# A Macaron transformer block on one core: seven products for the attention's values, plain tiles for x, and p2 on m1's bank

## The chip, the cores and the metric

The kernel runs on one core of a Trainium2 chip. The metric is the device time of one execution in microseconds. The kernel before took 1191.23 us, the median of 3 runs (1188.14 to 1192.05).

## What is computed

One block for 512 positions of 1024 features, all in float32: half a SwiGLU feed-forward block, a mixer of a short convolution and gated linear attention with four heads, half another feed-forward block, and a final RMS norm. Cut to what matters:

```python
D_MODEL, SEQ, D_FF = 1024, 512, 2816
GLA_HEADS, GLA_DK, GLA_DV, CHUNK = 4, 128, 256, 64

def swiglu(x, w_gu, w_down):
    g, u = jnp.split(x @ w_gu, 2, axis=-1)
    return (jax.nn.silu(g) * u) @ w_down

def hybrid_mixer(h, ...):
    z = h @ w_in
    cb, cc, cu, q, k, v, g_lr, r, ga, gb = jnp.split(z, SPLIT_POINTS, axis=-1)
    y_conv = (cb * causal_short_conv(cc * cu, conv_w)) @ w_out_conv
    log_a = jax.nn.log_sigmoid(g_lr @ gate_w_up + gate_b) / GATE_TAU
    o = gla_chunked(q, k, v, log_a)          # per head: decayed scores, states, outputs
    o = o * lax.rsqrt(jnp.mean(o * o, axis=-1, keepdims=True) + EPS)
    y_gla = (o.reshape(B, S, GLA_V) * gla_norm_g * jax.nn.silu(r)) @ w_out_gla
    merged = jax.nn.sigmoid(ga) * y_conv + jax.nn.sigmoid(gb) * y_gla
    return merged @ w_o

x = x + 0.5 * swiglu(rmsnorm(x, norm_ffn1_g), ffn1_w_gu, ffn1_w_down)
x = x + hybrid_mixer(rmsnorm(x, norm_mix_g), ...)
x = x + 0.5 * swiglu(rmsnorm(x, norm_ffn2_g), ffn2_w_gu, ffn2_w_down)
return rmsnorm(x, final_norm_g)
```

## The kernel before

**Matmuls.** Activations are kept transposed (features on the 128 partitions, the 512 positions beside them) in one large tile `X` of eight blocks. Each float32 operand is split into a high part, a ScalarE cast (L309 for a weight, into `wh`), and a low part, a VectorE subtraction (L310, into `wl`). A product is then three matmuls: high by high, high by low, low by high.

**Products and sets.** A *single* or a *group* is a plain product over all eight blocks of features. Most of the weights, though, go through *sets* of seven half-size products (the scheme of Strassen and Winograd), named m1, p2, q6, p5, q7, p4, p3. In an ordinary set (`Set.run`, matmuls at L501) one product is 24 matmuls of 128 by 256. Three PSUM banks take them: m1, then q6, q7 and p4 into b, p2 into a, p5 and p3 into c. What stands in b after m1, q6 and q7 is copied to SBUF by ScalarE (L506) before the next product writes there, and VectorE combines it later with another bank: m1 with p2's bank a, q6 and q7 with bank c. `order()` interleaves neighbours: the following set's m1 runs just before this set's p4, and its p2 between p4 and p3. The down projections use *wide* sets: matmuls of 128 by 512, two weight tiles to a product, order m1, p5, q6, p2, q7, p3, p4.

**Weights.** `PLAN` lists the tiles to load, `STEPS` the products that use them, in the order of use. `Weights.issue` runs two steps ahead of TensorE (PE): it casts and subtracts for a product, and asks for later loads. A set needs four loads and one sum tile, out of a pool `f` of ten tiles of 512 KB, so a load waits until an older tile is free. SyncE's queue (SP) issues the loads. They are asked for six steps ahead of the set's m1, and the sums of sub-blocks three steps ahead: s3 = a11 + a21 on VectorE; a21 += a22, and after the casts of m1 and p2, a11 += a21 and a12 += a11, as adding DMAs of GpSimd's queue (POOL, L287). Tiles of singles and groups are asked for by `fetch` a few steps ahead (four in the mixer). Each engine takes its instructions in a fixed order, by and large that in which they were written; DMA issues of SP may stand earlier.

**The mixer**, in its order on PE: the group of queries and keys of heads 0 and 1, with the gates' low-rank product; the values' first half (`v_half(0)`, by `mm_wide`: 96 matmuls of 128 by 512, L378 and others, recorded as L337 to L339 and L378 by form); singles for the queries and keys of heads 2 and 3, with the scores, state and output of head 0 between them; `v_half(1)`; twelve sets in the order of `MSETS` (ga and gb are the gates, conv the convolution, cb its gate, r the output gate) with the work of heads 1 to 3 hooked behind chosen products; w_out_conv in eight singles; two sets of w_out_gla; w_o. A head's work runs through `gates` (L1058 is its matmul on PE), `decays` (a scan and four exponentials, each function of ScalarE behind a table load), `scale`, `scores`, `state`, `output`, `squares`.

The matmuls of the values' halves read x as it is before the division by its root mean square; keys are therefore scaled by the square of that row (`row2`). The sets read `X` after VectorE has normalized it in place (L1032). Old x lies in device memory (`xs`) meanwhile: `reload`, a hook behind p3 of the first w_out_gla set, reads it into a new large tile with eight DMAs of POOL's queue (L1453), and `evac` (L1458) adds w_o's product to it.

Of the kernel before, what the change touches and what calls it, by code (L numbers as in the profile page):

```python
# [15 lines left out]
P = 128  # L16
S = 512
# [39 lines left out]


def wide(mat, kt, col):
    return [(mat, k0, 2, (col,), 512) for k0 in range(0, kt, 2)]  # L60
# [61 lines left out]
MSETS = [("ga", 0), ("gb", 0), ("conv", 0), ("ga", 1), ("conv", 1), ("gb", 1), ("conv", 2),  # L122
# [19 lines left out]
def ffn_plan(up, down, plain, slow):  # L142
# [6 lines left out]
    wide_sets(down)  # L149
# [4 lines left out]
def mixer_plan():  # L154
    units(group("w_in", KD, (QO, KO, QO + P, KO + P)))
    units(wide("w_in", KD, VO))
# [3 lines left out]
    units(wide("w_in", KD, VO + 512))  # L160
# [23 lines left out]
def block_kernel(ctx: ExitStack, tc: tile.TileContext, xT, vecs, gf, gup, wgl, wts, out):  # L184
# [58 lines left out]
    class Weights:  # L243
# [13 lines left out]
        def phase(self, early, first=6):  # L257
# [4 lines left out]
            for i in range(lo, self.end):  # L262
                n, p = STEPS[i]
                if p == "m1":
                    self.loads.setdefault(max(lo, i - first), []).append(n)
# [4 lines left out]
        def fetch(self, at):  # L270

            for n, p in STEPS[at : min(at + self.early, self.end)]:
# [78 lines left out]
    def mm_group(mat, kt, cols, ah, al, extra=None, slow=False):  # L351
        o = [MM() for _ in cols]
        n = len(cols)
        for u in group(mat, kt, cols, slow):
            h, l = W.take(u)
            for i in range(u[2]):
# [6 lines left out]
                if extra is not None:  # L363
                    extra(k)
        return o

    def mm_wide(mat, kt, col, ah, al, extra=None):
        o = [MM() for _ in range(NTB)]
        for u in wide(mat, kt, col):
            h, l = W.take(u)  # L370
            for i in range(u[2]):
                k = u[1] + i
                wh = h[:, i * 512 : (i + 1) * 512]
                wl = l[:, i * 512 : (i + 1) * 512]
                for t in range(NTB):
                    a = ah[k][:, t * P : (t + 1) * P]
                    b = al[k][:, t * P : (t + 1) * P]
                    nc.tensor.matmul(o[t], a, wh, start=k == 0, stop=False)  # L378
                    nc.tensor.matmul(o[t], a, wl, start=False, stop=False)
                    nc.tensor.matmul(o[t], b, wh, start=False, stop=k == kt - 1)  # L380
# [97 lines left out]
    class Set:  # L478
# [8 lines left out]
        def run(self, p):  # L487
# [16 lines left out]
            if p in ("m1", "q6", "q7"):  # L504
# [3 lines left out]
            self.done(self, p)  # L508

# [84 lines left out]

    def run_sets(make, ahead=2, hooks={}):
# [8 lines left out]
        for n, i in number.items():  # L604
            sets[n] = make(i)
        for i, (n, p) in enumerate(seq):
# [7 lines left out]
    def ffn(up, down, norm, nxt, plain, at):  # L614
# [917 lines left out]
```

## Time and profile before

| what | value |
|---|---|
| median of 3 runs | 1191.23 us |
| the profiled execution's own time | 1192.07 us |
| its span, first to last instruction | 1190.4 us |
| mean granted TensorE clock | 0.997 |
| first matmul of the mixer | at 343.2 us |
| first matmul of w_o | at 800.6 us |

All times on the page are within the span; 1.67 us of the profiled execution lie around it. In a row of a group, the numbers behind the bar are its busy time in us, the mean of one in ns, and the idle time of the engine just before its instructions with what ended it. In a row of a timeline, the first number is the start in us, the second how long the instruction was open, and the bracket behind it the idle time before it and its releaser. In the chain of waits, a row gives when a stretch of work began, how long it lasted, and the engine and line.

### The profile page before, as it was taken

The numbers are of one execution on the slowest core, as the hardware profiler recorded it, in microseconds if no ns is written. First come the engines' busy times: TensorE is split into PE (matmuls) and PEld (weight loads), VectorE is DVE, ScalarE is ACT, GpSimd is POOL, SyncE is SP. The second block draws the span as 40 slices with busy tenths as digits, with TensorE's granted clock in tenths as the row PEclk, the third lists the DMA queues.
The fourth block names the chain that finished last, engine by engine and source line by source line (L and its number), as shares of the span: only waits on it lengthen the run. The fifth ranks groups of instructions, "written<-read, shape, count | busy, mean of one in ns | idle before, by whom it ended". The sixth has DMA issues, their size and how long they took to land. (4 is left out here: it accounts for less than half of the span.)

```text
span 1190.4 us, 19195 instructions
## 1 busy us (share of the span) xinstructions
PE 1177.9 (99%) x7818; PEld 1085.6 (91%) x7818; DVE 878.5 (74%) x1044; ACT 625.5 (53%) x777; POOL 116.3 (10%) x155
## 2 busy tenths in 40 slices
PE   9999999999999999999999999999999999999997
PEld 8899999988788889999999998988889999998876
DVE  7976666897578765868688688676598666679955
ACT  6564454675245465646454566543345454566543
POOL 0011111101010001011111100200001101101100
PEclk9999999999999999999999999999999999999999
DMA  9477777678532325766877766741537777757721
GB/s 349 85 207 187 183 181 191 153 196 209 195 110 85 89 71 149 205 179 178 206 218 176 189 181 200 208 128 54 186 72 210 173 193 176 182 156 192 170 81 71
DMA packets 61224, 197.10 MB, mean 166 GB/s; under 512 B 6768, under 2 KB 13040, under 8 KB 61136
## 3 DMA queue, kind: packets, MB, share of 16 engines
q0 software_dynamic: 18560, 67.12, 30.7%
q1 hardware_dynamic: 37936, 124.27, 29.8%
q10 hardware_dynamic: 4640, 4.49, 1.2%
q8 instruction: 61, 1.00, 0.3%
q14 instruction: 27, 0.22, 0.1%
HBM read 124.55 MB, written 8.39 MB: 112 GB/s over the span
## 5 line engine op out<-in xcount | busy, mean ns | idle before, releaser
L501 PE MATMUL mm<-op,wh 128*128 128x256 f32 x3584 | 649.6, 284 | 2.8 <-ACT tp L506 2.8
L309 ACT CAST wh<-f 128x1024 fp32r<-128x1024 f32 (+1 forms) x335 | 350.1, 1046 | 439.4 <-PE mm L501 227.2
L501 PEld LDWEIGHTS mm<-op,wh 128*128 128x128 f32 x3584 | 560.2, 192 | 4.0 <-ACT tp L506 3.0
L310 DVE TENSOR_TENSOR wl<-f,wh 128x1024 fp32r<-128x1024 f32 (+1 forms) x335 | 406.9, 1217 | 182.2 <-ACT wh L309 176.5
L501 PE MATMUL mm<-op,wl 128*128 128x256 f32 x1792 | 508.1, 284 | 0.1
L501 PEld LDWEIGHTS mm<-op,wl 128*128 128x128 f32 x1792 | 344.0, 192 | 0.6 <-DVE wl L310 0.5
L287 POOL DMA_DIRECT2D f<-f x120 | 103.5, 866 | 922.1 <-DVE wl L310 477.1
L337 PE MATMUL mm<-op,wh 128*128 128x512 f32 x192 | 75.1, 391 | 0.0
L339 PE MATMUL mm<-op,wl 128*128 128x512 f32 x192 | 74.9, 390 | 0.0
L338 PE MATMUL mm<-op,wh 128*128 128x512 f32 x192 | 74.7, 389 | 0.0
L361 PE MATMUL mm<-op,wh 128*128 128x512 f32 x256 | 63.8, 391 | 0.2 <-DVE op L412 0.2
L791 PE MATMUL mm<-wl,op 128*128 128x512 f32 x160 | 62.6, 391 | 0.8 <-DVE wl L310 0.8
L789 PE MATMUL mm<-wh,op 128*128 128x512 f32 x160 | 62.3, 389 | 0.0
L793 PE MATMUL mm<-wh,op 128*128 128x512 f32 x160 | 62.2, 389 | 0.0
L361 PEld LDWEIGHTS mm<-op,wh 128*128 128x128 f32 x256 | 47.8, 188 | 10.6 <-issue 0.4
L506 ACT COPY tp<-mm 128x512 f32<-128x512 f32 x96 | 55.7, 580 | 1.9 <-DVE tp L1299 1.0
L296 DVE TENSOR_TENSOR f<-f,f 128x1024 f32<-128x1024 f32 x40 | 48.8, 1221 | 0.7
L339 PEld LDWEIGHTS mm<-op,wl 128*128 128x128 f32 x192 | 36.0, 188 | 7.5
L337 PEld LDWEIGHTS mm<-op,wh 128*128 128x128 f32 x192 | 36.1, 188 | 7.4
L338 PEld LDWEIGHTS mm<-op,wh 128*128 128x128 f32 x192 | 36.1, 188 | 7.4
L791 PEld LDWEIGHTS mm<-wl,op 128*128 128x128 f32 x160 | 30.0, 188 | 7.8 <-DVE wl L310 1.9
L789 PEld LDWEIGHTS mm<-wh,op 128*128 128x128 f32 x160 | 30.0, 188 | 6.3
(282 smaller groups left out, 1328.8 us busy)
## 6 DMA issues: line engine op xcount, KB each, us to landing
f<-wts SPq DMA_DIRECT2D x219, 512.0 KB, 4.4
f<-f POOLq DMA_DIRECT2D x120, 512.0 KB, 5.0
X<-xT SPq DMA_DIRECT2D x8, 256.0 KB, 5.2
xs<-X POOLq DMA_DIRECT2D x8, 256.0 KB, 2.3
ga<-tp ACTq DMA_DIRECT2D x8, 256.0 KB, 3.0
gb<-tp ACTq DMA_DIRECT2D x8, 256.0 KB, 4.9
tp<-ga SPq DMA_DIRECT2D x8, 256.0 KB, 6.0
X<-xs POOLq DMA_DIRECT2D x8, 256.0 KB, 7.5
```

The costliest lines, as they stand in the source:

```text
L287: nc.gpsimd.dma_start(out_, a, accum_op=ALU.add)
L309: self.cast = nc.scalar.copy(h[:, :w], raw[:, :w]).ins
L310: nc.vector.tensor_tensor(out=l[:, :w], in0=raw[:, :w], in1=h[:, :w].bitcast(F32), op=ALU.subtract)
L337: nc.tensor.matmul(o, wh, ah, start=first, stop=False)
L338: nc.tensor.matmul(o, wh, al, start=False, stop=False)
L339: nc.tensor.matmul(o, wl, ah, start=False, stop=last)
L361: nc.tensor.matmul(o[c], w[:, s : s + P], a[k], start=k == 0 and j == 0, stop=k == kt - 1 and j == 2)
L501: nc.tensor.matmul(to, ww[:, s], aa[:, t], start=fresh and k == 0 and e == 0 and j == 0, stop=k == 3 and j == 2, skip_group_check=True)
L506: nc.scalar.copy(v, o)
L789: nc.tensor.matmul(o[t], bh[:, s], wh, start=fresh and k == 0, stop=False, skip_group_check=True)
L791: nc.tensor.matmul(o[t], bh[:, s], wl, start=False, stop=False, skip_group_check=True)
L793: nc.tensor.matmul(o[t], bl[:, s], wh, start=False, stop=k == 3, skip_group_check=True)
```

## The change

Five parts, of which the diff shows the core.

- The values are computed as one wide set of seven products (`natural_set`, cut out of the down projections' code), on the normalized x. The four singles now stand before the set, and head 0's gates, decays and scaling between them. The scores of head 0 follow the set's m1, and the rest of heads 0 to 3 is hooked over sets 0 to 8. Keys are scaled by the row alone. The order of `MSETS` changes in four places.
- The loads of an ordinary set that follows a wide one are asked for eight steps ahead instead of six; inside sets, `fetch` looks three steps ahead.
- In every ordinary set but the first of a run (`forked`), ScalarE's copy of m1 goes into bank a, and p2 accumulates onto it there. The VectorE addition of m1 to p2 goes. Bank a takes p2's result through `first()`.
- Old x is read by SP into eight 128 by 512 tiles that are free by then (`x_old`), one behind each single of w_out_conv, and `evac` adds from there.
- Outputs of the heads go to their own large tile at once; `move` goes.

```diff
-MSETS = [("ga", 0), ("gb", 0), ("conv", 0), ("ga", 1), ("conv", 1), ("gb", 1), ("conv", 2),
+MSETS = [("ga", 0), ("gb", 0), ("ga", 1), ("conv", 0), ("gb", 1), ("conv", 1), ("conv", 2),
...
-def wide_sets(mat):
-
-    for w in range(WIDE):
+def wide_sets(mat, n=1, col=0):
+
+    for w in range(n):
         subs = []
         for u in range(2):
             subs.append(len(PLAN))
-            PLAN.extend((mat, 8 * w + 4 * j + 2 * u, 2, (512 * c,), 512)
+            PLAN.extend((mat, 8 * w + 4 * j + 2 * u, 2, (col + 512 * c,), 512)
...
     units(group("w_in", KD, (QO, KO, QO + P, KO + P)))
-    units(wide("w_in", KD, VO))
     for h in (2, 3):
         units(single("w_in", KD, QO + h * P))
         units(single("w_in", KD, KO + h * P))
-    units(wide("w_in", KD, VO + 512))
+    wide_sets("w_in", 1, VO)
...
+                    after = STEPS[i - 1][1] is not None and PLAN[STEPS[i - 1][0]][4] > HW
+                    wait = PLAN[n][4] == HW and after
+                    self.loads.setdefault(max(lo, i - (8 if wait else first)), []).append(n)
...
+            inside = at < self.end and STEPS[at][1] is not None
+            for n, p in STEPS[at : min(at + (3 if inside else self.early), self.end)]:
                 if p is None and n not in self.raw:
                     self.raw[n] = self.dma(n)
-                elif p is not None and STEPS[at][1] is None:
...
+                elif p is not None and not inside:
...
-            if p in ("m1", "q6", "q7"):
+            if p == "m1" and self.forked:
+                self.bank["a"] = MM()
+                nc.scalar.copy(self.bank["a"], o)
+            elif p in ("m1", "q6", "q7"):
...
+        def first(self):
+
+            if self.forked:
+                return self.bank["a"]
+            t = T()
+            nc.vector.tensor_tensor(out=t, in0=self.bank["a"], in1=self.v["m1"], op=ALU.add)
+            return t
...
+    def natural_set(ops, banks, done, ahead=1):
+
+        used = {"a"}
+        for at, p in enumerate(SEQ):
+            for q in SEQ[at : at + ahead + 1]:
+                ops.make(q)
+            n = {"m1": "b", "p2": "a", "q6": "b", "p5": "c", "q7": "b", "p4": "b", "p3": "c"}[p]
+            fresh = n not in used
+            used.add(n)
+            o = banks[n]
+            bh, bl = ops.get(p)
+            for u in range(2):
+                h, l = W.take()
+                for i in range(2):
+                    k = 2 * u + i
+                    wh, wl = (a[:, i * 512 : (i + 1) * 512] for a in (h, l))
+                    for t in range(2):
+                        s = slice(k * HW + t * P, k * HW + (t + 1) * P)
+                        nc.tensor.matmul(o[t], bh[:, s], wh, start=fresh and k == 0,
+                                         stop=False, skip_group_check=True)
+                        nc.tensor.matmul(o[t], bh[:, s], wl, start=False, stop=False,
+                                         skip_group_check=True)
+                        nc.tensor.matmul(o[t], bl[:, s], wh, start=False, stop=k == 3,
+                                         skip_group_check=True)
+            done(p, o)
...
+            sets[n].forked = i > 0
...
-                    g1 = T()
-                    nc.vector.tensor_tensor(out=g1, in0=bank["a"], in1=v["m1"], op=ALU.add)
-                    nc.scalar.activation(g1, g1, AF.Silu)
-                    s.g1 = g1
+                    s.g1 = T()
+                    nc.scalar.activation(s.g1, s.first(), AF.Silu)
...
-            mul(QK[h][:, 1], o, row2)
+            mul(QK[h][:, 1], o, row)
...
-        v_half(0, one({1: [lambda: gates(0)], 3: [decays], 5: [lambda: scale(0)]}))
-        oq = mm_single("w_in", KD, QO + 2 * P, xh, xl)
-        scores(0)
-        evac_q(2, oq)
-        ok = mm_single("w_in", KD, KO + 2 * P, xh, xl)
-        state(0)
-        evac_k(2, ok)
-        xo.make("m1")
-        oq = mm_single("w_in", KD, QO + 3 * P, xh, xl)
-        output(0)
-        evac_q(3, oq)
-        ok = mm_single("w_in", KD, KO + 3 * P, xh, xl)
-        squares(0)
-        gates(1)
-        evac_k(3, ok)
-        xo.make("p2")
-        v_half(1, one({1: [decays], 3: [lambda: scale(1), lambda: xo.make("p5")],
-                       5: [lambda: xo.sum("q6")]}))
...
+        def v_done(p, o):
+            for t in range(2):
+                if p == "m1":
+                    nc.scalar.copy(A[t], o[t])
+                elif p == "p2":
+                    nc.scalar.copy(vt[0][t], o[t])
+                elif p == "p5":
+                    nc.scalar.copy(vt[1][2 + t], o[t])
+                elif p == "q6":
+                    nc.scalar.copy(vt[0][2 + t], o[t])
+                elif p == "q7":
+                    v = vt[1][2 + t]
+                    nc.vector.scalar_tensor_tensor(out=v, in0=o[t], scalar=-1.0, in1=v,
+                                                   op0=ALU.mult, op1=ALU.subtract)
+                elif p == "p3":
+                    v = vt[0][2 + t]
+                    nc.vector.tensor_tensor(out=v, in0=o[t], in1=v, op=ALU.add)
+                else:
+                    nc.scalar.activation(vt[1][t], o[t], AF.Copy, scale=-1.0)
+            if p == "m1":
+                scores(0)
+
+        steps = [lambda: gates(0), decays, lambda: scale(0)]
+        for h in range(2, HEADS):
+            for c, evac in ((QO, evac_q), (KO, evac_k)):
+                o = mm_single("w_in", KD, c + h * P, xh, xl)
+                if steps:
+                    steps.pop(0)()
+                if c == QO:
+                    xo.make("p2" if h == 3 else "m1")
+                elif h == 2:
+                    xo.sum("p5")
+                evac(h, o)
+        A = [MM(), MM()]
+        natural_set(xo, {"a": A, "b": [MM(), MM()], "c": [MM(), MM()]}, v_done)
+        OB = big("O").rearrange("p (h e) t -> p h e t", e=2)
+        O.extend(OB[:, h] for h in range(HEADS))
...
+        chain = [(0, "q6", state, 0), (0, "q7", output, 0), (0, "p3", squares, 0),
+                 (1, "q6", gates, 1), (1, "q7", None, 1), (1, "p4", scale, 1),
+                 (2, "q6", scores, 1), (2, "q7", state, 1), (2, "p4", output, 1),
+                 (3, "q6", squares, 1), (3, "q7", gates, 2), (3, "p3", None, 2),
+                 (4, "q6", scale, 2), (4, "p3", scores, 2), (5, "q6", state, 2),
+                 (5, "p4", output, 2), (5, "p3", squares, 2), (6, "q6", gates, 3),
+                 (6, "q7", None, 3), (6, "p4", scale, 3), (7, "q6", scores, 3),
+                 (7, "q7", state, 3), (7, "p4", output, 3), (8, "q6", squares, 3)]
+        for n, p, f, h in chain:
+            hooks[n, p] = [(lambda f=f, h=h: f(h)) if f else decays]
...
-                    s.t1 = T()
-                    nc.vector.tensor_tensor(out=s.t1, in0=bank["a"], in1=v["m1"], op=ALU.add)
+                    s.t1 = s.first()
+                    if s.forked:
+                        s.t1 = T()
+                        nc.scalar.copy(s.t1, bank["a"])
...
+                    if p == "p2" and s.forked:
+                        r = T()
+                        nc.scalar.activation(r, t, func or AF.Copy)
+                        t = r
...
+        x_old = [QK[2 + i][:, j] for i in range(2) for j in range(2)] + [
+            pools["g"].tile([P, S], F32, tag=t, name=f"{t}_x") for t in ("sc", "reset", "gup_w", "glr")]
...
+            nc.sync.dma_start(x_old[d], xs[d])
...
-                nc.gpsimd.dma_start(x[k], xs[k])
...
-            nc.vector.tensor_tensor(out=x[d], in0=o, in1=x[d], op=ALU.add)
+            nc.vector.tensor_tensor(out=x[d], in0=o, in1=x_old[d], op=ALU.add)
```

What the change moves is seen on three engines. The numbers behind the names count tiles.

**VectorE where the values begin.** Before, behind the row of 1/rms and the first evacuations (`wl`: the low part of a weight tile; `X`, `op`: x normalized in place, and the low part of an operand made from it; `g0`, `g1`: head 0's gates):

```order
L310 TENSOR_TENSOR wl572_3776<-f539_3599,wh571_3775 128x1024
L1032 SCALAR_TENSOR_TENSOR X_88<-X_88,vec_84,row551_3713 128x512 x4
L310 TENSOR_TENSOR wl576_3814<-f548_3659,wh575_3813 128x1024
L1062 TENSOR_SCALAR g1_562_3762<-aux573_3803,vec_84 128x512
L550 TENSOR_TENSOR op601_4022<-X_88,op600_4021 128x1024
L1032 SCALAR_TENSOR_TENSOR X_88<-X_88,vec_84,row551_3713 128x512 x2
```

After, the rows that lead up to the set's m1 (`wl584`, its second weight tile), p5 (`wl594`, `wl596`) and q6 (`wl602`, `wl604`); `qk503` is a query or key of heads 2 and 3, `sc` the scores:

```order
L1001 SCALAR_TENSOR_TENSOR qk503_3470<-mm577_3856,row554_3716 128x512
L308 TENSOR_TENSOR wl584_3906<-f538_3595,wh583_3905 128x1024
L541 TENSOR_TENSOR op581_3900<-X_88,op580_3899 128x1024
L455 TENSOR_TENSOR qk503_3470<-mm582_3904,row554_3716 128x512
L541 TENSOR_TENSOR op592_3942<-X_88,op591_3941 128x1024
L308 TENSOR_TENSOR wl594_3946<-f535_3590,wh593_3945 128x1024
L308 TENSOR_TENSOR wl596_3962<-f540_3599,wh595_3961 128x1024
L1105 COPY_PREDICATED sc_3475<-mask_3480,aux597_3979 128x512
L522 SCALAR_TENSOR_TENSOR X_88<-X_88 128x4x256
L308 TENSOR_TENSOR wl602_4000<-f533_3586,wh601_3999 128x1024
L308 TENSOR_TENSOR wl604_4016<-f538_3595,wh603_4015 128x1024
```

The low parts of the operands (`op581`, `op592`) and the sum for q6 (L522, made from the normalized `X`) now stand among the low parts of the values' weights. Before, the values read operands that had been split earlier, and only their weights stood here in front of PE.

**ScalarE ahead of the copy of m1 of set 7** (conv 3). Before (`CAST wh`: a weight's high part; the `COPY` rows are copies of b, the last one that of m1):

```order
L309 CAST wh868_6041<-f798_5521 128x1024
L309 CAST wh873_6074<-f830_5775 128x1024
L506 COPY tp870_6069<-mm838_5815 128x512
L309 CAST wh876_6105<-f796_5517 128x1024
L506 COPY tp875_6103<-mm872_6073 128x512
```

After (L1058 and L1071 to L1075: `gates` and `decays` of a head; the last row is m1's copy, now into a bank, `mm865`):

```order
L1058 ACT_TABLE_LOAD
L1058 ACTIVATE g0_563_3762<-g0_563_3762 128x512
L307 CAST wh863_6001<-f819_5683 128x1024
L489 COPY tp860_5989<-mm827_5722 128x512
L1071 ACT_TABLE_LOAD
L1071 ACTIVATE sm_3767<-g0_563_3762 128x8
L1072 ACTIVATE sm_3767<-g0_563_3762 128x8
L307 CAST wh866_6032<-f787_5432 128x1024
L1073 ACTIVATE g3_566_3765<-g1_564_3763 128x512
L1075 ACTIVATE g2_565_3764<-g2_565_3764 128x512
L1074 ACTIVATE g1_564_3763<-g1_564_3763 128x512
L486 COPY mm865_6030<-mm862_6000 128x512
```

Head 3's exponentials have moved ahead of that copy; before, all heads were done by then.

**The reading of x.** Before, on POOL's queue between the sums of the two w_out_gla sets (`f<-f`: an adding DMA of L287):

```order
L287 DMA f1031_7321<-f1033_7325 128x1024
L287 DMA f1032_7323<-f1031_7321 128x1024
L1453 DMA X2_7920<-xs_3473 128x512 x8
L287 DMA f1062_7531<-f1064_7535 128x1024
L287 DMA f1063_7533<-f1062_7531 128x1024
```

After, on SP's queue among the weights of sets 7 to 10 (`f<-wts`: a load; `qk502`, `gup_w`, `glr`, `reset`: the plain tiles):

```order
L281 DMA f819_5683<-wts 128x1024
L1422 DMA qk502_3469<-xs_3458 128x512 x2
L281 DMA f820_5685<-wts 128x1024
L281 DMA f821_5687<-wts 128x1024
L281 DMA f853_5952<-wts 128x1024
L281 DMA f854_5954<-wts 128x1024
L281 DMA f855_5956<-wts 128x1024
L1422 DMA gup_w_x_7295<-xs_3458 128x512
L1422 DMA glr_x_7296<-xs_3458 128x512
L281 DMA f856_5958<-wts 128x1024
L1422 DMA reset_x_7294<-xs_3458 128x512
L281 DMA f884_6216<-wts 128x1024
```

The eight reads have left POOL's queue and stand on SP's, among the loads for four sets of the mixer, earlier than the code names them (behind the singles of w_out_conv).

More of the change, by code (lines that the diff above doesn't have):

```diff
@@ L362, in mm_group @@
                                          stop=k == kt - 1 and j == 2)
[L363 to L380, printed above, removed]
                 if extra is not None:
@@ L807, in run_wide @@
                         add(0, 1, t, o[t], 0.5)
+            natural_set(downs[w], banks, done)
             return banks["c"]
@@ L1203, in mixer @@
-        OB = []
-        def move():
-            OB.append(big("O").rearrange("p (h e) t -> p h e t", e=2))
-            for h in range(2):
-                nc.scalar.copy(OB[0][:, h], O[h])
-            for h in range(HEADS):
-                O[h] = OB[0][:, h]
+        def v_done(p, o):
[19 more added lines that the diff above has]
+                scores(0)
@@ L1296, in quarter @@
                 return None
+            if p == "p2":
+                return s.first()
             t = T()
@@ L1301, in quarter @@
             else:
-                nc.vector.tensor_tensor(out=t, in0=bank["a" if p == "p2" else "c"],
-                                        in1=v["m1" if p == "p2" else "q6"], op=ALU.add)
+                nc.vector.tensor_tensor(out=t, in0=bank["c"], in1=v["q6"], op=ALU.add)
             return t
@@ L1451, in reload @@
             x[:] = [XS[-1][:, k] for k in range(KD)]
-            for k in range(KD):
-                nc.gpsimd.dma_start(x[k], xs[k])
         run_sets(lambda i: Set(oo, gla_done(i)), hooks={(0, "p3"): [reload]})
```

61 lines of the change are left out of this document (8 added, 53 removed).

## The prediction

> **What bounds the kernel now.** The page's head comes first, then the waits of TensorE.
>
> ```profile
> span 1190.4 us, 19195 instructions
> PE 1177.9 (99%) x7818; PEld 1085.6 (91%) x7818; DVE 878.5 (74%) x1044; ACT 625.5 (53%) x777; POOL 116.3 (10%) x155
> ```
> ```profile
> PE mm L501 <- ACT tp L506: 2.8, 1, 2.8
> PE aux L228 <- POOL ones L225: 1.1, 1, 1.1
> PE mm L791 <- DVE wl L310: 0.8, 1, 0.8
> PE aux L791 <- DVE wl L310: 0.5, 1, 0.5
> ```
>
> PE is busy in 99% of the span and waits five times in all, under 6 us. So time is lost only where a product is taken away from PE or where a wait of PE goes, and won back by nothing else: faster VectorE work is worth nothing by itself. The busy time of a matmul overlaps its neighbour's, so the rate has to be read from a stretch. The chain of waits gives it for the sets (256 columns each):
>
> ```profile
> 914.69 20.16 PE mm L501 x168
> ```
>
> That is 0.120 us for one, 2.88 us for a product of 24. The stretches table gives it for the two passes over the values (512 columns), which are the group below, three lines of 64 matmuls:
>
> ```profile
> 371.38:393.39 22.01, 22.01 (x98) 1.00 0.23 72
> 423.44:445.26 21.82, 21.82 (x98) 1.00 0.30 67
> ```
> ```profile
> L378 PE MATMUL mm<-wh,op 128*128 128x512 f32 x64 | 24.9, 390 | 0.0
> ```
> ```profile
> 376.82 0.40 PE L1058 MATMUL aux<-glr,gup_w 96*128 96x512 f32 x1
> 377.05 0.40 PE L378 MATMUL mm<-wh,op 128*128 128x512 f32 x1
> ```
>
> The first pass holds one foreign matmul (376.82, 0.23 us). 22.01 - 0.23 + 21.82 = 43.60 us for 192 matmuls, or 0.227 us each, at a granted clock of 1.00 and with no wait. That 0.227, not the 390 ns of the row, is the price of a matmul taken away.
>
> **Term 1, the values: -5.45 us.** Two passes of 96 matmuls become seven products of 24, 168 in all, same shape. 24 fewer at 0.227 us is 5.45 us, all on PE, which sets the end. The Trainium skill ("TensorE: Matmul & The Clock Gate", Back-to-back issue gap) gives a sustained rate of about 131 ns for 512 columns, by which the saving would be 3.1 us; the 22 us of these passes for 96 matmuls contradict it here, and the measurement decides.
>
> **Term 2, the reading of x: -2.85 us.** PE's longest wait is followed back through GpSimd's and ScalarE's timelines and the chain.
>
> ```profile
> 759.85 4.31 POOL L1453 DMA_DIRECT2D X<-xs  x8 [6.09 <-DVE op L550]
> 767.07 0.89 POOL L287 DMA_DIRECT2D f<-f  x1 [2.92 <-DVE wl L310]
> ```
> ```profile
> 767.07 9.21 DMA f<-f
> ```
> ```profile
> f<-f POOLq DMA_DIRECT2D x120, 512.0 KB, 5.0
> ```
> ```profile
> 776.38 1.05 ACT L309 CAST wh<-f 128x1024 fp32r<-128x1024 f32 x1 [4.63 <-DMA f<-f]
> ...
> 791.73 1.04 ACT L309 CAST wh<-f 128x1024 fp32r<-128x1024 f32 x1 [4.27 <-DMA f<-f]
> 792.68 0.58 ACT L506 COPY tp<-mm 128x512 f32<-128x512 f32 x1
> ```
> ```profile
> 793.31 0.58 PE L501 MATMUL mm<-op,wh 128*128 128x256 f32 x1 [2.85 <-ACT tp L506]
> ```
>
> Eight reads of x go out of POOL's queue just ahead of an adding transfer (a11 += a21 of the second set of w_out_gla). That add takes 9.21 us instead of the median 5.0. The split of q6 waits for it (776.38), everything behind slips, the second add (for p3) lands late (791.73), and the copy of q7 stands behind that split on ScalarE, which works in order. PE waits 2.85 us for the copy. In the change POOL issues none of these reads. SP issues eight, into tiles that are free, among the loads of sets 7 to 10 and 40 us or more before use. Without them the add lands 4.2 us sooner, at the median, the split of q6 is no longer late, and the copy comes some 3 us sooner, about when PE wants it. I take the whole 2.85; the ends are 0 (VectorE's own work there still holds it up) and 3.1, with the 0.26 that the matmul after the wait lost. Eight more issues cost SP some 0.4 us each beside waits for slots that last longer.
>
> **Term 3, the start of the values: +1.6 us.** The four q and k singles now come first (96 matmuls, as the old first pass), so the values begin at the same 393.4, but VectorE has less time for what they need.
>
> ```profile
> 374.27 1.23 DVE L310 TENSOR_TENSOR wl<-f,wh 128x1024 fp32r<-128x1024 f32 x1
> 375.41 2.73 DVE L1032 SCALAR_TENSOR_TENSOR X<-X,vec,row 128x512 f32<-128x512 f32 x4
> 378.15 1.23 DVE L310 TENSOR_TENSOR wl<-f,wh 128x1024 fp32r<-128x1024 f32 x1
> ...
> 389.02 0.69 DVE L475 TENSOR_TENSOR y<-g,y 128x512 f32<-128x512 f32 x1
> ...
> 392.24 1.22 DVE L310 TENSOR_TENSOR wl<-f,wh 128x1024 fp32r<-128x1024 f32 x1
> ```
> ```profile
> 393.39 0.39 PE L337 MATMUL mm<-op,wh 128*128 128x512 f32 x1
> ```
>
> Start to start a 1024-wide operation costs 1.14 us, a 512-wide normalization 0.68, the eight products of the decay scaling 3.22. The order of the change puts after 374.27, up to and with the low part of the second half of m1's weights: eight 1024-wide (9.1), seven normalizations (4.8), seven other 512-wide at about 0.61 (4.3), the scan (1.2) and the scaling (3.3), which is 22.7 us, and some 0.6 of waiting for ScalarE's operand cast, behind a table load. That ends at 397.6. PE wants it at its second matmul of the second half, 393.39 + 12 x 0.227 + 0.23 = 396.3. So PE waits 1.3 us. The following p5 is covered by the scores of head 0, which now stand between m1 and p5 on PE. At q6 the low part of its operand is about 0.3 us late, since its cast stands behind a weight cast that waits for p5's first half. Ends: 0 (the same work gave PE no wait in the old order) and 4 (all of ScalarE's waits on top).
>
> **Term 4, the end of the values: +0.7 us.** The loads of the first set behind the values need slots that the values free late. On POOL the add of the second following set stands ahead of a11 += a21 of the first; it needs a load into the slot that p4's first half frees. The landing times are those of the same seven products at the end of the first feed-forward block, adds first, then loads:
>
> ```profile
> DMA to landing us min/median/max: 4.5/4.8/5.5
> ```
> ```profile
> DMA to landing us min/median/max: 4.9/5.6/6.5
> ```
>
> From the start of step 10 of the values to the start of q6 PE needs 4 x 2.72 + 2 x 2.88 = 16.6 us. The way takes 2.5 (two evacuations and the low part that reads the slot), 5.6 (load), 0.9 (issue), 5.5 (two adds at once), 1.05 and 0.95 (casts of q6 and p5) and 0.58 (copy of m1, behind them): 17.1, and 0.2 of handovers. So q6 is 0.7 us late. Asked for six steps ahead the first set's loads would stand two steps of 2.72 us later, so the eight steps keep this from being some 5 us. Ends: 0 and 4.4, with an add of 9.21.
>
> **Term 5, m1 into p2's bank: +1.5 us.** The copy costs the same into a bank as into a tile; 18 VectorE additions go in the feed-forward blocks but for one each, and as many again in the mixer, none of them waited for by PE. What is new is the deadline: p2 waits for the copy of m1, which until now q6 waited for.
>
> ```profile
> L797 ACT COPY mm<-mm x4: 570/570/570, 236.7 to 1078.7; 128x512 f32<-128x512 f32 x4
> ```
> ```profile
> L691 DVE TENSOR_TENSOR tp<-mm,tp x18: 682/691/693, 57.3 to 1068.9; 128x512 f32<-128x512 f32 x18
> ```
> ```profile
> 648.68 1.05 ACT L309 CAST wh<-f 128x1024 fp32r<-128x1024 f32 x1 [1.35 <-PE mm L501]
> 649.63 0.58 ACT L506 COPY tp<-mm 128x512 f32<-128x512 f32 x1
> ```
>
> In an ordinary set the cast starts when m1 ends and the copy is done 1.5 us later, while p4 covers 2.88: a margin of 1.35 us. Where a head's gates stand before it, the margin is gone:
>
> ```profile
> 482.16 0.40 PE L1058 MATMUL aux<-glr,gup_w 96*128 96x512 f32 x1
> ```
> ```profile
> 641.47 1.34 ACT L1243 ACTIVATE tp<-y,vec 128x512 f32<-128x512 f32 x2
> ...
> 493.52 0.59 ACT L506 COPY tp<-mm 128x512 f32<-128x512 f32 x1 [0.99 <-DVE tp L1299]
> ```
>
> There the copy ended at 494.1, 11.95 us behind the gates' matmul; p2 would have begun 0.23 + 4 x 2.88 = 11.75 behind it. In the order of the change set 7 has the same chain, with two convolution steps (1.34) and one cast more (0.95) ahead of the copy, and without the 0.99 of waiting: 13.25, so p2 waits 1.5. Set 2 has neither and ends at about 11.0, in time. Ends: 0 and 3.5 (both sets, one cast more each).
>
> **What costs nothing.** Fetching three steps ahead inside sets is three and two steps of 2.72 us, 13.6, before use, against a landing of 5.6; if that cover went, one late load would cost a few us. O written to its own tile saves ScalarE two copies that nothing waits for. The heads' chain, spread over nine sets instead of six, adds no work to PE.
>
> **The sum.** The profiled execution took 1192.07: 1192.07 - 5.45 - 2.85 + 1.6 + 0.7 + 1.5 = 1187.57. It stood 0.84 above the median of the runs (1191.23), so the forecast is **1186.7 us**, 0.4% below.
>
> **Rivals.** *All waits are covered* (terms 3 to 5 at nothing): 1182.9. For it: in the old order much of the same work was hidden; against it: the sums above have no slack. *The traffic only moves*: 2 MB of x still go through, now beside the adds of sets 7 to 10 and of the loads there, and a wait like the 2.85 stays: 1189.6. The Trainium skill ("DMA: Bandwidth & Descriptors", Issuing engines are not separate DMA queues) says that transfers from any engine's queue interleave on the same 16 engines, and by that rule the change of queue alone would bring nothing. Against the rival: an ordinary add is issued some 9 us before the split that reads it, against 5.0 to land. *The waits are all at their upper bounds*, or nearly: about 1191. *Slower*: ScalarE's queue sets the pace of the mixer. If in six of its eleven such sets the copy of m1 comes as late as in set 7, instead of one, that adds 5 x 1.5, and with terms 3 and 4 doubled 2.3 more: 1196.5. It decides from a copy 2.88 us behind m1's end; in the order most sets have one cast ahead of it, which speaks against.
>
> **How the numbers follow.** About 0.3% (3.6 us) is what a measurement of this kernel can tell from no change: below 1187.7 is faster, above 1194.8 slower. Forecast 0.50 (spread 1184.8 to 1188.9, three fifths of it faster), covered 0.22, traffic 0.10, upper bounds 0.10, slower 0.08. Faster 0.30 + 0.22 = 0.52, slower 0.08, same the remaining 0.40. The range from 1182.0 to 1191.5 takes in all but the slower case and some edges.
>
> **What would show it.** Right: 168 matmuls in the values in about 38 us; no PE wait near the end of w_out_gla; a wait of 1 to 2 us on a low part at the values' second step; PE waiting for ScalarE's copy of m1 at set 7's p2. Wrong: PE waits for those copies in many sets, adds of 9 us in sets 7 to 10, or a PE busy in the values without any gap.

## The result and the profile after

The changed kernel took 1201.41 us, the median of 4 runs (1200.69 to 1203.1), against 1191.64 us (4 runs, 1188.14 to 1192.96) for the kernel before: a ratio of 1.0086, 95% interval [1.0067, 1.0105]. It is slower by 9.8 us. 1186.7 was forecast, 1182.0 was the lower end of the range and 1191.5 the upper one. The profiled execution of after took 1201.73 us, its span 1200.0.

The page's head, then the waits of TensorE after the change (total, times, longest, in us):

```profile
span 1200.0 us, 19158 instructions
PE 1178.1 (98%) x7794; PEld 1081.8 (90%) x7794; DVE 870.6 (73%) x1027; ACT 632.6 (53%) x790; POOL 117.1 (10%) x153
```
```profile
PE mm L606 <- DVE wl L308: 6.2, 7, 1.5
PE mm L481 <- ACT tp L489: 3.5, 2, 3.1
PE mm L604 <- ACT wh L307: 1.7, 2, 1.1
PE aux L223 <- POOL ones L220: 1.1, 1, 1.1
PE mm L481 <- ACT mm L486: 1.1, 1, 1.1
PE aux L606 <- DVE wl L308: 0.9, 2, 0.5
PE mm L481 <- DVE wl L308: 0.4, 2, 0.2
```

24 matmuls are gone (7794 for 7818), and the waits have grown from under 6 us to about 15. The largest group is in lines 604 and 606, which the values share with the down projections; all of its waits lie in the down projections (242 to 310 us and 1086 to 1155 us). Two landmarks place the loss. The gate's first matmul stands near the mixer's start (L999 before, L995 after), the weight loads of the ordinary sets those of the second feed-forward block (L501 before, L481 after); the last two numbers of a row are the first and last start. Before:

```profile
L999 PE MATMUL aux<-op,g x8: 389/395/481, 349.8 to 370.9; 128*96 128x512 f32 x8
L501 PEld LDWEIGHTS mm<-op,wh x1008: 187/192/192, 888.0 to 1072.7; 128*128 128x128 f32 x168
```

After:

```profile
L995 PEld LDWEIGHTS aux<-op,g x8: 159/161/163, 355.7 to 376.7; 128*96 128x96 f32 x8
L481 PEld LDWEIGHTS mm<-op,wh x1008: 187/192/193, 892.0 to 1076.7; 128*128 128x128 f32 x168
```

The first block costs 5.9 us more (349.8 to 355.7); 0.9 of it is there already ahead of the down projection, where the same adding transfer is issued at 220.92 instead of 220.01. From there to the second block's sets it is 538.2 before and 536.3 after, 1.9 less. The sets take 184.7 in both. What follows them to the span's end takes 117.7 before and 123.3 after, 5.6 more. So the blocks lost: the second one behind its ordinary sets, at the down projection, whose arithmetic the change doesn't touch. That the mixer gained 1.9 us is not shown by this: in a run below that has the mixer of the kernel before (before_with_adds_swapped), the same stretch took 535.2 (356.3 to 891.5).

The timeline of TensorE at the second block's first wide set shows two of these waits (before, the same set ran without one):

```profile
1086.11 0.49 PE L604 MATMUL mm<-wh,op 128*128 128x512 f32 x1 [0.68 <-ACT wh L307]
1087.37 0.50 PE L606 MATMUL mm<-wl,op 128*128 128x512 f32 x1 [0.76 <-DVE wl L308]
```

In the first block, ScalarE stood idle ahead of the split of p5's second half, waiting for an adding DMA. The same split before, then after:

```profile
234.68 1.06 ACT L309 CAST wh<-f 128x1024 fp32r<-128x1024 f32 x1 [0.32 <-PE mm L793]
```
```profile
240.91 1.04 ACT L307 CAST wh<-f 128x1024 fp32r<-128x1024 f32 x1 [5.11 <-DMA f<-f]
```

These adds are POOL's. The two kernels queue them differently at the first wide set. Before (`f320` and `f327` are a21 of the first and second half, `f318` and `f325` their a11):

```
L287 DMA f320_2351<-f321_2353 128x1024
L287 DMA f327_2389<-f328_2391 128x1024
L287 DMA f318_2347<-f320_2351 128x1024
L287 DMA f325_2385<-f327_2389 128x1024
```

After (`f314`, `f321` are the a21; `f312`, `f319` the a11):

```
L285 DMA f314_2338<-f315_2340 128x1024
L285 DMA f312_2334<-f314_2338 128x1024
L285 DMA f321_2376<-f322_2378 128x1024
L285 DMA f319_2372<-f321_2376 128x1024
```

The first half's a11 += a21 has come ahead of the second half's a21 += a22. It needs the first half's sum, so POOL, which works in order, waits for that sum to land, and the second half's sum waits behind it. POOL's timeline before, and the time to landing of its first row, the second half's sum:

```profile
229.57 0.86 POOL L287 DMA_DIRECT2D f<-f  x1 [2.60 <-DVE f L296]
231.33 0.86 POOL L287 DMA_DIRECT2D f<-f  x1 [0.89 <-DVE hid L700]
```
```profile
DMA to landing us min/median/max: 4.5/4.5/4.5
```

After, with the time to landing of both adds of its row:

```profile
232.25 1.75 POOL L285 DMA_DIRECT2D f<-f  x2 [4.36 <-DMA f<-f]
```
```profile
DMA to landing us min/median/max: 4.6/6.3/8.0
```

Before, the second half's sum was issued at 229.57 and landed at 234.1, ahead of the split. After, it went second of two at 232.8, 0.5 us behind another add, and took 8.0 us: it landed at 240.8, just as ScalarE's split began. What reordered the queue was to be found by experiment.

### The profile page after: what moved, and what is told of

It is laid out like the page before. It is cut to its first block, busy times and chain, and to the rows that moved or that the text cites. A ratio compares the mean times of both kernels' runs of the same rounds, so it can differ in the third digit from the quotient of the medians.

```text
span 1200.0 us, 19158 instructions
## 1 busy us (share of the span) xinstructions
PE 1178.1 (98%) x7794; PEld 1081.8 (90%) x7794; DVE 870.6 (73%) x1027; ACT 632.6 (53%) x790; POOL 117.1 (10%) x153
## 5 line engine op out<-in xcount | busy, mean ns | idle before, releaser
L481 PE MATMUL mm<-op,wh 128*128 128x256 f32 x3584 | 650.7, 284 | 4.6 <-ACT tp L489 3.5
L307 ACT CAST wh<-f 128x1024 fp32r<-128x1024 f32 (+1 forms) x341 | 356.1, 1046 | 440.0 <-PE mm L481 209.0
L308 DVE TENSOR_TENSOR wl<-f,wh 128x1024 fp32r<-128x1024 f32 (+1 forms) x341 | 413.6, 1217 | 218.2 <-ACT wh L307 213.0
L481 PEld LDWEIGHTS mm<-op,wh 128*128 128x128 f32 x3584 | 559.7, 192 | 6.7 <-ACT tp L489 4.1
L481 PE MATMUL mm<-op,wl 128*128 128x256 f32 x1792 | 508.6, 284 | 0.5 <-DVE wl L308 0.4
L481 PEld LDWEIGHTS mm<-op,wl 128*128 128x128 f32 x1792 | 343.5, 192 | 1.2 <-DVE wl L308 1.1
L285 POOL DMA_DIRECT2D f<-f x126 | 108.7, 866 | 944.5 <-DVE wl L308 515.9
L606 PE MATMUL mm<-wl,op 128*128 128x512 f32 x216 | 85.3, 395 | 6.3 <-DVE wl L308 6.2
L604 PE MATMUL mm<-wh,op 128*128 128x512 f32 x216 | 84.3, 392 | 1.7 <-ACT wh L307 1.7
L608 PE MATMUL mm<-wh,op 128*128 128x512 f32 x216 | 84.2, 390 | 0.0
L359 PEld LDWEIGHTS mm<-op,wh 128*128 128x128 f32 x256 | 48.2, 190 | 10.4
L606 PEld LDWEIGHTS mm<-wl,op 128*128 128x128 f32 x216 | 40.5, 188 | 17.7 <-DVE wl L308 9.6
L294 DVE TENSOR_TENSOR f<-f,f 128x1024 f32<-128x1024 f32 x42 | 51.2, 1221 | 2.6 <-DMA f<-wts 1.2
L604 PEld LDWEIGHTS mm<-wh,op 128*128 128x128 f32 x216 | 40.5, 188 | 11.4 <-ACT wh L307 3.0
L608 PEld LDWEIGHTS mm<-wh,op 128*128 128x128 f32 x216 | 40.5, 188 | 8.4 <-DVE op L541 0.4
```

What stands on the lines that cost most here:

```text
L285: nc.gpsimd.dma_start(out_, a, accum_op=ALU.add)
L294: nc.vector.tensor_tensor(out=s3, in0=a11, in1=a21, op=ALU.add)
L307: self.cast = nc.scalar.copy(h[:, :w], raw[:, :w]).ins
L308: nc.vector.tensor_tensor(out=l[:, :w], in0=raw[:, :w], in1=h[:, :w].bitcast(F32), op=ALU.subtract)
L359: nc.tensor.matmul(o[c], w[:, s : s + P], a[k], start=k == 0 and j == 0, stop=k == kt - 1 and j == 2)
L481: nc.tensor.matmul(to, ww[:, s], aa[:, t], start=fresh and k == 0 and e == 0 and j == 0, stop=k == 3 and j == 2, skip_group_check=True)
```

## The experiments

Each kernel is named by its label; "edge" is a note to the builder that one DMA is to be queued behind another, with no wait for its end. Ratios are to the kernel before in the same batch.

**The order of the adds, put back** (adds_as_before_in_ffn). The edit, in the kernel after:

```diff
-                self.add(a21, a22)
+                i = self.add(a21, a22)
+                self.sum2 = i if PLAN[n][4] > HW else None
...
-                self.add(a11, a21)
+                i = self.add(a11, a21)
+                if self.sum2 is not None:
+                    follow(i, self.sum2)
```

> The kernel after, with one edge more: the adding DMA of m1 (a11 += a21) of a wide set's first half is queued on GpSimd behind a21 += a22 of its second half, as it stands in the kernel before. The order of every other engine is that of the kernel after. Theory A, the order of the adds costs the time in the down products: the waits of TensorE at 240 to 248 us (4.1 in all) and at 1085 to 1092 us (3.7) go to under 0.5 each, those in the second wide sets may go back with them (2.0 more), and the time is 1191.5 to 1193.6. Theory B, m1 copied into p2's bank costs it by itself (ScalarE's order, the banks): the waits stay and the time is 1200.5 to 1202.

Measured 1191.01 (10 runs), ratio 0.9998 [0.9986, 1.0011]: 10.4 us below the kernel after, a little more than the 7.8 to 9.9 that theory A gave. Its waits of TensorE:

```profile
PE mm L489 <- ACT tp L497: 3.4, 2, 3.1
...
PE mm L614 <- DVE wl L314: 1.0, 2, 0.6
PE aux L614 <- DVE wl L314: 0.9, 2, 0.4
```

The waits for the low parts in the down projections fell from 7.1 to 1.9, those for high parts are gone. POOL's first two adds of the set, and the time to landing of the first (the second half's sum):

```profile
231.09 0.86 POOL L290 DMA_DIRECT2D f<-f  x1 [3.14 <-DVE f L299]
232.50 0.86 POOL L290 DMA_DIRECT2D f<-f  x1 [0.56 <-DMA f<-f]
```
```profile
DMA to landing us min/median/max: 4.6/4.6/4.6
```

Issued 1.7 us sooner, the sum landed 5.2 us sooner (235.6). The order of PE, VectorE, ScalarE and SP is that of the kernel after, and on POOL one pair of adds is exchanged in each block, so the order on POOL alone did it.

**m1 copied into a tile in the feed-forward blocks** (plain_m1_in_ffn). `forked` is false there, and true in the mixer.

> The kernel after with m1 copied into a tile and added by VectorE in the feed-forward blocks, as before; the mixer keeps the copy into the bank. Theory A: the order of GpSimd's queue falls back by itself, so 1191.5 to 1193.6, the same as with the edge within 0.5. Theory B: the same time here, but not with the edge alone. Theory C, neither (the loads asked for three steps ahead instead of five, the other traffic): 1200.5 to 1202 in both.

Measured 1191.36 (10 runs), ratio 1.0002 [0.9993, 1.0012]. With VectorE's addition back, the builder queues the adds as before without any edge. So the copy into the bank caused the loss, but only through that order: the run above keeps the copy and loses nothing. Which half of it moves the builder, the copy into the bank or the missing addition, was not separated.

**The kernel before, with the adds swapped** (before_with_adds_swapped).

```diff
-                self.add(a21, a22)
+                i = self.add(a21, a22)
+                if PLAN[n][4] > HW and len(self.two) < 2:
+                    self.two.append(i)
...
-                self.add(a11, a21)
+                i = self.add(a11, a21)
+                if len(self.two) == 2:
+                    follow(self.two[1], i)
+                    self.two += [None]
```

> The kernel before with nothing changed but that order: a21 += a22 of the second half of each block's first wide set queued behind a11 += a21 of the first half. Theory A: two waits of about 4 us appear in the first wide sets, and up to 1 us each behind them: 1199.0 to 1201.5. Theories B and C: 1191 to 1192.

Measured 1200.4 (4 runs), ratio 1.0075 [1.0054, 1.0095], 9.3 us slower, with no other part of the change in it. In the first block, which took 6.5 us more (356.3 for 349.8, of which 1.0 stands ahead of the down projection), POOL's order is the only difference; in the second the builder also exchanged a few neighbours on ScalarE's and VectorE's queues. POOL's row is the one of the kernel after:

```profile
232.25 1.75 POOL L293 DMA_DIRECT2D f<-f  x2 [4.31 <-DVE hid L711]
```

```profile
PE mm L802 <- DVE wl L318: 4.5, 7, 0.9
PE mm L800 <- ACT wh L317: 2.1, 3, 0.9
PE mm L512 <- ACT tp L517: 1.6, 1, 1.6
...
PE aux L802 <- DVE wl L318: 0.5, 1, 0.5
```

The waits in the down projections rose from 1.3 (0.8 and 0.5) to 7.1, while the one in w_out_gla, where nothing was changed, fell from 2.8 to 1.6. There are eleven of them, each under 1 us, in place of two blocks of 4. Behind the two in the second block's first wide set the granted TensorE clock also fell (start and end of the stretch, its length, TensorE's busy time and matmuls, granted clock, DMA share and GB/s):

```profile
1087.73:1091.15 3.42, 3.42 (x9) 0.50 0.57 99
```

Sign and total are theory A's, the split among the sets is not.

**The mixer's adds in the order of the code** (adds_in_turn_in_mixer). Each adding DMA of the mixer is queued behind the one that the code names before it.

> The kernel after with the mixer's adding DMAs queued in the order in which the code names them: at the end of the values, a11 += a21 and a12 += a11 of the first set ahead of a21 += a22 of the second. Theory A, the first set's a11 += a21 is late because another add is issued just ahead of it and lands beside it (7.61 us): it lands in 4.5 to 5.5, TensorE's wait of 3.1 us at q6 goes to under 1, and the time is 1198.2 to 1199.5. Rival: it is late because its input is, and ScalarE's queue holds the rest: the wait stays at 2.5 or more, 1201 to 1202.

Measured 1196.22 (5 runs), ratio 1.0044 [1.0028, 1.0059]: 5.2 us below the kernel after, against 1.9 to 3.2 expected. At the end of the values the kernel after had this wait at q6 of the first set; POOL's row and the times to landing of its two adds stand below it:

```profile
449.94 0.50 PE L481 MATMUL mm<-op,wh 128*128 128x256 f32 x2 [3.14 <-ACT tp L489]
...
438.82 1.76 POOL L285 DMA_DIRECT2D f<-f  x2 [8.61 <-DVE f L294]
```
```profile
DMA to landing us min/median/max: 6.0/6.8/7.6
```

With the edges, a11 += a21 goes alone:

```profile
439.09 0.86 POOL L290 DMA_DIRECT2D f<-f  x1 [9.61 <-DVE wl L317]
```
```profile
DMA to landing us min/median/max: 4.6/4.6/4.6
```

It lands at 443.7 instead of 447.3, and the wait is 0.14 us. The mechanism holds. Some 2 us of the 5.2 are not that wait, and the granted clock shows most of them in the profiled executions. TensorE's next 4 us behind the wait in the kernel after, a later stretch of it, and the same place in this run and in adds_as_before_in_ffn:

```profile
449.94:453.94 4.00, 4.00 (x21) 0.57 1.01 217
455.00:459.00 4.00, 4.00 (x31) 1.00 0.74 263
```
```profile
446.26:450.26 4.00, 4.00 (x30) 1.00 1.06 199
```
```profile
445.12:449.12 4.00, 4.00 (x30) 1.00 1.01 206
```

Behind its wait of 3.14 us the kernel after has a clock of 0.57, and its next 20 matmuls take 4.0 us; here they take 2.5. In adds_as_before_in_ffn the wait is as long (3.06 us), but the clock behind it stayed at 1.00. So a wait of 3 us was followed by another loss of 1.5 us in one execution, and by none in another.

**Both orders at once** (adds_in_both).

> The kernel after with both orders of adding DMAs: in the feed-forward blocks as before, in the mixer as the code names them. If the two losses are separate, 1201.4 - 10.4 - 5.2 = 1185.8, so 1185 to 1187. Rival: a part of the 5.2 that the mixer's order brought alone is the same time as that in the feed-forward blocks (only 3.0 us of TensorE's waits were seen to go at the values' end), and the two together give 1187.5 to 1189.

Measured 1187.84 (10 runs), ratio 0.998 [0.9968, 0.9993]: 13.6 us below the kernel after, not 15.6, so the rival has it by number. The slow stretch shows where the overlap can lie: it is in the profiled execution of the kernel after, and in neither of the profiles with one order alone, so its 1.5 us count in both losses. This version is faster than the kernel before.

**Set 7 without the copy into the bank** (both_and_set7_alone), on top of both orders:

> As the kernel before it in this list, but set 7 of the mixer copies m1 into a tile, and VectorE adds it, so that q6 and not p2 waits for the copy. Theory, the wait of 1.1 us at p2 of set 7 (1.27 us of lost cadence) is that copy behind head 3's decays: the wait goes and the time is 1.0 to 1.4 below the kernel before it in this list. Rival: ScalarE is late there for everything, and the next product waits instead: within 0.4 of it.

Measured 1187.48 (10 runs), ratio 0.9976 [0.9965, 0.9986], 0.4 below the kernel above, less than two sets of runs of one program differ by (see the next run): the rival. The wait at p2 is gone, and two others came:

```profile
601.09 0.38 PE L494 MATMUL mm<-op,wl 128*128 128x256 f32 x1 [0.57 <-DVE wl L319]
...
608.38 0.39 PE L494 MATMUL mm<-op,wl 128*128 128x256 f32 x1 [0.38 <-DVE wl L319]
```

**Six steps instead of eight** (both_with_six_steps), on top of both orders: `i - first` for `i - (8 if wait else first)`.

> As the first kernel of this list, but the loads of the first set behind the values are asked for six steps ahead instead of eight. Theory of the prediction (its term 4): they come two steps of 2.72 us later, and TensorE waits 3 to 5 us at the start of the first set. Rival: those loads wait for slots that the values free late, however early they are asked for: within 0.5 of the first kernel.

Measured 1187.02 (10 runs), ratio 0.9973 [0.9963, 0.9983]. That is 0.8 below adds_in_both, but the edit did nothing: the two traces hold the same instructions, with the same operands and waits, on every queue. The builder makes one program of both, and 0.8 us is what two sets of ten runs of one program differ by. So the earlier request brings nothing here, and the prediction's 5 us for it were wrong; what loads that did come later would cost was not tested.

**The kernel before with the plain tiles for x alone** (before_with_plain_x). The eight reads move from `reload` to SP, as in the change.

> The kernel before with the reading of x alone changed: SyncE reads it into the eight free tiles, and GpSimd's eight reads go. Theory (term 2): the wait of 2.85 us in w_out_gla goes to about 0.5, and the time is 1188.2 to 1189.0. Rival, the traffic only moves: 1190.8 to 1191.5.

Measured 1189.12 (10 runs), ratio 0.9989 [0.9978, 0.9999], 1.8 us faster by the medians, just above the range that the theory gave and well below the rival's. The add that took 9.21 us goes out at the same time (767.1) and lands in 6.3, and the wait in w_out_gla, 2.85 before, is down to

```profile
790.86 0.39 PE L501 MATMUL mm<-op,wh 128*128 128x256 f32 x1 [0.36 <-ACT tp L506]
```

**Head 3's chain one or two products later** (both_and_head3_later), on top of both orders: gates behind (6, q7), decays behind (6, p3), scale behind (7, q6), and so on to squares behind (8, p3).

> The kernel adds_in_both with head 3's hooks moved one or two products later: gates behind q7 of set 6 and decays behind its p3, as head 2 has them. ScalarE then copies m1 of set 7 ahead of the decays. If the wait at set 7 (1.26 us) comes from these exponentials, it goes and no other takes its place: 1186.2 to 1187.0. Rival: as with set 7 alone, another wait there of about the same size: 1187.5 to 1188.2.

Measured 1186.64 (9 runs), ratio 0.9972 [0.9962, 0.9982]. The wait at set 7 is gone and none took its place there, so it was the exponentials. A gain in time is not shown: the program of adds_in_both came to 0.998 and 0.9973 in its two sets of runs, this one to 0.9972 and, in the next, 0.9968, and the intervals overlap.

**The same with the longer look of `fetch`** (both_head3_fetch_early):

> As the kernel before it in this list, with fetch looking as far ahead inside sets as before (four steps in the mixer, five in the feed-forward blocks). I priced the shorter look at nothing, its loads waiting for slots either way: within 0.6 of the kernel before it. Rival: the late low parts at the end of the second wide sets (2.0 us in the second block) come from it: 1 to 2 us faster.

Measured 1186.56 (6 runs), ratio 0.9968 [0.9957, 0.9979]: no difference, and again the traces hold the same instructions on every queue. The look changes nothing in the program, so the late low parts in the second wide sets, which are still there, don't come from it.

**Both orders, and no copies into banks at all** (both_without_copies_into_banks):

> The kernel adds_in_both with m1 copied into tiles and added by VectorE in all sets, as before. If the copy into the bank brings nothing, as TensorE never waited for those additions, the time is within 0.6 of adds_in_both (1187.84), or up to 1.3 faster where p2 of set 7 need not wait. Rival: the additions now delay low parts on VectorE: 1 to 2 us slower.

Measured 1189.04 (11 runs), ratio 0.9992 [0.9983, 1.0001]. By the ratios that is 1.4 us slower than adds_in_both (0.998), and 2.3 slower than the same program's second set of runs (0.9973), but the intervals overlap or touch; it points to a gain of 1 to 2 us from the copies and doesn't prove it. Its waits for low parts in the sets are the longer ones (2.0 us in five waits, against 0.4 in two), yet with those for ScalarE's copies TensorE's waits in the ordinary sets come to 2.6 us in both kernels, so they don't show where a gain would come from:

```profile
PE mm L494 <- DVE wl L319: 2.0, 5, 0.6
```

## Why the prediction was wrong

The step that failed is in term 5: of the VectorE additions that go in the feed-forward blocks it said "none of them waited for by PE", and it priced the part at the mixer's set 7 alone. The additions were indeed not waited for. But without them, and with m1's copy in the bank, the builder gives POOL's queue another order at each block's first wide set, and that cost 10.4 us. The rows of POOL's order would have shown it beforehand; the prediction looked at POOL for the reads of x and for the end of the values only. The rival for "slower" had the sign right and the place wrong (ScalarE's queue in the mixer).

That step is not the whole error. With it undone the change stands at 0.9998 of the kernel before, where a gain of 4.5 us was forecast. Of the rest, term 4 shows the largest miss.

The terms one by one:

- **Term 1**, forecast -5.45. The stretch of the values took 41.56 us, with 21 foreign matmuls:

```profile
399.37:440.93 41.56, 41.50 (x189) 33.74 (x188) 36.55 (x37) 25.58 (x30) 5.25 (x7) 1.00 0.60 157
```

Those 21 took some 2.9 us by the timeline (402.54 to 403.25 and 405.65 to 407.88), which leaves 38.6 for the 168, against 43.6 for 192 before: -5.0. Right.

- **Term 2**, forecast -2.85. TensorE's wait fell from 2.85 to 0.35:

```profile
798.76 0.51 PE L481 MATMUL mm<-op,wh 128*128 128x256 f32 x2 [0.35 <-ACT tp L489]
```

By the run of its own 1.8 went, or 1.3 by the ratio, with an interval of 0.1 to 2.6. Right in mechanism, and the rival by which the traffic only moves has fallen. The size leaves out the clock: in the profile of the kernel before it was 0.58 in the 4 us behind that wait, and 1.00 there with the plain tiles. No run tests the rule that stood beside it (the Trainium skill, "DMA: Bandwidth & Descriptors", Issuing engines are not separate DMA queues), since the reads changed their time along with their queue.

- **Term 3**, forecast +1.6. TensorE shows no wait there. VectorE was late much as worked out: its low part ended at 403.2, and by the prediction, with the shift of 6 us from the first block, at 403.6. But the order on TensorE has pieces of head 0's scores ahead of the matmul that reads it:

```profile
401.97 1.22 DVE L308 TENSOR_TENSOR wl<-f,wh 128x1024 fp32r<-128x1024 f32 x1
...
402.54 0.38 PE L1102 MATMUL aux<-y 128*128 128x128 f32 x2
402.85 0.33 PE L1103 MATMUL aux<-g 128*64 128x64 f32 x2
403.25 0.50 PE L606 MATMUL mm<-wl,op 128*128 128x512 f32 x1
```

The prediction put the scores behind m1 as a whole.

- **Term 4**, forecast +0.7, upper end 4.4. The wait was 3.1. The mechanism was the one named, a sum of the second set queued ahead of a11 += a21. What was mis-sized is the landing of the two adds issued one behind the other: 5.5 us in the sum, where a11 += a21 took 7.6, while the load ahead of them took the 5.6 that was put down. The 1.5 us at the lower clock behind the wait come on top.
- **Term 5 in the mixer**, forecast +1.5 at p2 of set 7. The wait was 1.1, behind head 3's exponentials:

```profile
610.65 0.58 ACT L486 COPY mm<-mm 128x512 f32<-128x512 f32 x1
...
611.28 0.39 PE L481 MATMUL mm<-op,wh 128*128 128x256 f32 x1 [1.11 <-ACT mm L486]
```

Right in place and size, and both_and_head3_later shows the cause. The prediction's count of the additions was off without effect on this: m1 is copied into a bank 28 times in all (L486), 16 in the feed-forward blocks and 12, not as many again, in the mixer.

- **Nothing for the look of `fetch`**: held, as far as tested: on top of both orders the program is the same with either look.

In the mixer this makes -5.0 - 2.5 + 3.1 + 1.1 = -3.3 where the landmarks show -1.9; each of the two profiles has one stretch at the lower clock in the mixer, so these cancel, and the rest was not found.

With the adds queued as before in the feed-forward blocks alone, the change comes to 1191.01, and with the mixer's in turn too to 1187.84, 1.1 above the forecast. That this is so near is in part luck: term 4's wait is 0.7 us there, as forecast, but only because the add that the forecast put ahead of a11 += a21 now stands behind it, and term 3's 1.6 never came.

## What to carry to other kernels

Where a builder orders a queue, an edit on one engine can reorder another engine's queue in a stage that the edit was not about; compare the issue order of every queue before pricing an edit at nothing, the DMA queues first. In a queue that works in order, a transfer that needs the result of the one just ahead of it belongs behind all that are ready. And when a large loss appears in lines that were not changed, undo the order alone, with everything else kept: one edge told the cause from the edit that had brought it about. An edit may also leave the program as it was: two of the runs above measured one program twice, which is seen by comparing their instructions, not their times.

## What was not expected of the hardware

Adding transfers of 512 KB behind one another nearly take turns. One alone landed in 4.5 to 4.6 us. Of two issued 0.5 us apart in the changed kernel the first landed in 4.6 all the same, and the second in 8.0, which is 4.0 us behind the first. At 1.4 us apart (4.6 and 7.1, adds_as_before_in_ffn) and at 1.8 (4.5 and 6.7, the kernel before) the second also landed 4.0 and 3.9 us behind the first. At the values' end, beside loads, the two took 6.0 and 7.6, 2.5 us apart. So the second sum of the first block, issued 1.7 us later and second instead of first, landed 5.2 us later.

TensorE's clock can fall behind a wait of 3 us. Over the 4 us behind the waits of 3.14 us (after), 2.85 (before) and 2.81 (plain_m1_in_ffn) the granted clock was 0.57, 0.58 and 0.61, and behind one of 3.06 (adds_as_before_in_ffn) it was 1.00. That the wait brings the lower clock about is likely from the order in time, but what decides whether it comes is open.
